# FFN of a decoder block in three chunks of hidden columns, with two of each eight pairs of contraction tiles as seven block products instead of eight

## The chip, the cores and the metric

The kernel runs on one core of one Trainium2 chip, as one launch. The metric is the device time of the launch in microseconds (us), as the median of several runs; lower is better.

## What is computed

One decoder block on 272 tokens (16 meta tokens, which the output drops, and 256 of the input) with a model width of 2,048, all in float32. Cut to what matters:

```python
hn = rms_norm(h, norm_mix_g)
u, gb_in, gc_in, v_in, ga_lin, gbr_lin = split(hn @ w_in)
y_a = grouped_matmul(causal_multiscale_pool(u), pool_w) * pool_scale
y_b = (gb_in * causal_depthwise_conv(gc_in * v_in, conv_w)) @ conv_out_w
g_a, g_b = split(sigmoid(concat(ga_lin, gbr_lin) + b_gate))
h = h + (g_a * y_a + g_b * y_b) @ w_o
hn = rms_norm(h, norm_ffn_g)
gate, up = split(hn @ w_gate_up)            # 2048 -> 2 x 5632
h = h + (silu(gate) * up) @ w_down          # 5632 -> 2048
out = rms_norm(h, norm_final_g)[:, 16:]
```

## The kernel before

**Matmuls in three passes.** A float32 operand is split into two parts, hi (rounded to the matmul's type) and lo (the rest), and a product is hi*hi + hi*lo + lo*hi: three matmuls of 128 x 128 by 512 columns that add up in one PSUM bank. In `mm_rows` (lines 149 to 155) the activations are the stationary operand (128 contraction rows x 128 tokens) and the weights the moving one (128 x 512 columns); lines 153, 154 and 155 are the three passes.

**The stream of weights.** All weights lie in memory in the order of use, as chunks of eight 128 x 128 tiles (512 KB). `load` (line 101) brings one into one of 5 raw buffers, on SP's queue. `split_weights` (line 108) makes hi on ScalarE (line 115) and lo on VectorE (line 116) into a ring of 3 hi and 3 lo tiles. `next_tile` and `next_block` call `advance` at each new chunk, which issues loads up to 4 chunks ahead and splits up to 2 ahead. A chunk is two blocks of 512 columns, so in the row-wise stages it feeds 2 contraction tiles x 2 token halves x 3 passes = 12 matmuls.

**The stages.** First the input projection and the two mixers, with the weights stationary (`pair`, `flat`, lines 189 to 200). Then, row-wise by `rows` (line 157): gates and mixers' outputs in 4 column chunks, the output projection in 4 (line 412), FFN up in FC = 11 chunks of 512 gate and 512 up columns (lines 437 to 448), and FFN down in 4 chunks of 512 columns over all FT = 44 contraction tiles (lines 464 and 465). `rows` takes one bank for each of the two token halves and steps through the contraction tiles; banks rotate among 8. The results of a stage lie by token, and the next needs them by contraction: `turn` (line 234) transposes them on TensorE (line 242) and `narrow` or `split` (lines 212 to 222) make hi and lo. `turn_a(c - 1)` stands between the gate and the up half of chunk c; the last turn of a stage stands `BW` = 4 contraction tiles ahead of the end of the first row pass of the next (argument `before`), which needs its result at once.

**Around it.** The FFN norm is applied late: `r2`, one over the root mean square, is found after the output projection and multiplied into the gate and up sums (lines 441, 442, 447). In FFN down every chunk is added to `hn` (line 467 by `binary`, line 209), squared on ScalarE (468) and multiplied by the final gain on GpSimd, for the last chunk on VectorE (469). In the last chunk `HELD` = 6 contraction tiles are done for token half 0 first and then for half 1, so that the first half's scaling and its store lie beside matmuls.

What sets the order: a scheduler of the framework orders each engine's instructions when the kernel is built, by the written order and by what is ready; at run time each engine keeps that order.

Of the kernel before, what the change touches and what calls it, by code (L numbers as in the profile page):

```python
# [31 lines left out]
LOADS_AHEAD = 4  # L32
SPLITS_AHEAD = 2
# [14 lines left out]
SPAD = 34  # L48
# [5 lines left out]
def block_kernel(ctx: ExitStack, tc: tile.TileContext, xT, xn, gfin, consts, spread, weights, out):  # L54
# [3 lines left out]

    nc = tc.nc
# [3 lines left out]
    wraw = ctx.enter_context(tc.tile_pool(name="wraw", bufs=5))  # L63
    whi = ctx.enter_context(tc.tile_pool(name="whi", bufs=3))
    wlo = ctx.enter_context(tc.tile_pool(name="wlo", bufs=3))
    ps = ctx.enter_context(tc.tile_pool(name="ps", bufs=8, space=PSUM))
    scope = ExitStack()
    spool = scope.enter_context(tc.tile_pool(name="spool", bufs=KT))
# [13 lines left out]
    def bank():  # L82
        return ps.tile([P, 512], F32, name="acc")
# [14 lines left out]
    raws, splits = {}, {}  # L98
# [9 lines left out]
    def split_weights(c, parts=1):  # L108
        raw = raws.pop(c)
        hi = whi.tile([P, CH * P], F32R, name="hi")  # L110
        lo = wlo.tile([P, CH * P], F32R, name="lo")
        step = CH * P // parts
        for s in range(0, CH * P, step):
            q = slice(s, s + step)
            nc.scalar.copy(out=hi[:, q], in_=raw[:, q])  # L115
            nc.vector.tensor_tensor(out=lo[:, q], in0=raw[:, q], in1=hi[:, q], op=ALU.subtract)  # L116
        splits[c] = hi, lo

    state = {"tile": 0, "loaded": 0, "split": 0}

    def advance(c):
        while state["loaded"] < min(c + LOADS_AHEAD + 1, n_chunks):
            load(state["loaded"])
            state["loaded"] += 1
        while state["split"] < min(c + SPLITS_AHEAD + 1, n_chunks):
            split_weights(state["split"])
            state["split"] += 1

    def next_tile():
        c, i = divmod(state["tile"], CH)  # L130
        if i == 0:
            advance(c)
            splits.pop(c - 1, None)
        state["tile"] += 1
        hi, lo = splits[c]
        return hi[:, i * P : (i + 1) * P], lo[:, i * P : (i + 1) * P]

    def next_block():
        c, i = divmod(state["tile"], CH)
        assert i % BW == 0  # L140
        if i == 0:
            advance(c)
            splits.pop(c - 1, None)
# [82 lines left out]
    slots = {"a": 20, "b": 16, "x": 8}  # L226

    def slot(tag, shape, dt=F32):
        return apool.tile(shape, dt, name="act", tag=tag, bufs=slots[tag])
# [4 lines left out]
    def turn(src, c, make):  # L234

        for j in range(0, BW, 2):
            p = bank()
            for i in range(2):
                for b in range(NB):
                    q = i * SEQ + b * P  # L240
                    f = slice((j + i) * P, (j + i + 1) * P)
                    nc.tensor.transpose(out=p[:, q : q + P], in_=src[b][:, f], identity=ident)  # L242
            for i in range(2):
                make(c * BW + j + i, p[:, i * SEQ : (i + 1) * SEQ])
# [47 lines left out]
    for c in range(KT * HEAD // CH):  # L292
        k0 = c * CH // HEAD
        k1 = k0 + CH // HEAD
        xsp += [wide(xall[:, k, :], col(C_GMIX, k)) for k in range(k0, k1)]
        split_weights(c, 2 if c == 0 else 1)
        state["split"] = c + 1
# [72 lines left out]
    def turn_s(c):  # L370
        turn(s_rows.pop(c), c, lambda j, p: ss.append(narrow(p, "a")))
# [28 lines left out]
    hpool = scope.enter_context(tc.tile_pool(name="hpool", bufs=KT))  # L400
    tmr = scope.enter_context(tc.tile_pool(name="tmr", bufs=1))
    hn = one.tile([P, NB, D], F32, name="hn", tag="stream")
    nc.gpsimd.dma_start(out=hn, in_=xn)
    sq2 = one.tile([P, NB, NC], F32, name="sq2")
    r2 = one.tile([P, NB], F32, name="r2")
    hsp = []

    def turn_h(c):
        turn([hn[:, b, c * BC : (c + 1) * BC] for b in range(NB)], c,
             lambda j, p: hsp.append(split(hpool.tile([P, 2, SEQ], F32R, name="hp"), p, col(C_GFFN, j))))  # L410

    for c in range(NC):
        for b, p in enumerate(rows(ss, n=KT, before=(lambda: turn_s(NC - 1)) if c == 0 else None)):
            h = hn[:, b, c * BC : (c + 1) * BC]
            binary(h, p, h, ALU.add)
            junk = tmr.tile([P, BC], F32, name="junk", tag="row", bufs=4)
            nc.scalar.activation(out=junk, in_=h, func=AF.Square, accum_out=sq2[:, b, c : c + 1])
        if c > 0:
            turn_h(c - 1)
    st2 = one.tile([P, NB, SPAD], F32, name="st2")  # L420
    for b in range(NB):
        ms, sd, y, y2, m2 = [st2[:, b, i : i + 1] for i in range(5)]
        binary(ms, sq2[:, b, 0:1], sq2[:, b, 1:2], ALU.add)
        binary(ms, ms, sq2[:, b, 2:3], ALU.add)
        binary(ms, ms, sq2[:, b, 3:4], ALU.add)
        mean(ms, ms)
        rsqrt(r2[:, b : b + 1], ms, sd, y, y2, m2)


    acts, a_rows = [], {}  # L430

    def turn_a(c):
        order = [t for t in slots for _ in range(slots[t])]
        turn(a_rows.pop(c), c, lambda j, p: acts.append(narrow(p, order[j])))

    for c in range(FC):
        gs = []
        for b, p in enumerate(rows(hsp, n=KT, before=(lambda: turn_h(NC - 1)) if c == 0 else None)):
            r = r2[:, b : b + 1]
            g = tmr.tile([P, BC], F32, name="gs", tag="row", bufs=4)  # L440
            nc.scalar.activation(out=g, in_=p, func=AF.Sigmoid, scale=r)
            nc.vector.scalar_tensor_tensor(out=g, in0=p, scalar=r, in1=g, op0=ALU.mult, op1=ALU.mult)
            gs.append(g)
        if c > 0:
            turn_a(c - 1)
        for b, p in enumerate(rows(hsp)):
            nc.vector.scalar_tensor_tensor(out=gs[b], in0=p, scalar=r2[:, b : b + 1], in1=gs[b], op0=ALU.mult, op1=ALU.mult)
        a_rows[c] = gs


    first = rows(acts, n=FT, before=lambda: turn_a(FC - 1))
    scope.close()
    fin = ctx.enter_context(tc.tile_pool(name="fin", bufs=1))
    gf = fin.tile([P, D], F32, name="gf")
    nc.gpsimd.dma_start(out=gf, in_=gfin)
    hg = fin.tile([P, NB, D], F32, name="hg")
    junk = fin.tile([P, BC], F32, name="junk")
    part = fin.tile([P, NB, NC], F32, name="part")
    base = fin.tile([P, NB], F32, name="base")
    st = fin.tile([P, NB, 6], F32, name="st")  # L460
    preload = fin.tile([P, 1], F32, name="preload")
    for c in range(NC):
        q = slice(c * BC, (c + 1) * BC)
        last = c == NC - 1
        for b, p in enumerate(first if c == 0 else rows(acts, HELD if last else 0)):
            h = hn[:, b, q]
            binary(h, p, h, ALU.add)
            nc.scalar.activation(out=junk, in_=h, func=AF.Square, accum_out=part[:, b, c : c + 1])
            (nc.vector if last else nc.gpsimd).tensor_tensor(out=hg[:, b, q], in0=h, in1=gf[:, q], op=ALU.mult)
            if c == 0 and b == 1:  # L470
                nc.scalar.activation(out=preload, in_=ones[:, 0:1], func=AF.Sqrt)
            if c == NC - 2:

                s = base[:, b : b + 1]
# [89 lines left out]
```

## Time and profile before

| | |
|---|---|
| runs | 1491.25 us median of 3 (1491.2 to 1491.41) |
| profiled execution | 1491.44 us |
| its span | 1489.6 us |
| TensorE matmul / weight load busy | 1478.4 us / 1276.2 us |
| VectorE / ScalarE / GpSimd busy | 861.3 / 656.8 / 15.6 us |
| read from memory | 285.38 MB |

The span goes from the first to the last instruction of the profiled execution; its time has 1.84 us around it. Matmuls are pipelined: each one's recorded time covers its way through the array, so recorded times of neighbours overlap and add up to more than the span would hold. What one costs is seen from the distance of the starts.

### The profile page before, as it was taken

Reading aid. Unit: us, or ns where it says so; the run is one execution under the profiler, and the core shown is the slowest. Engines: PE = TensorE matmul, PEld = TensorE weight load, DVE = VectorE, ACT = ScalarE, POOL = GpSimd, SP = SyncE. Lnnn points to the kernel's source line nnn. Section 1 sums busy time; section 2 is a strip of 40 time slices with the busy share of each in tenths; the row PEclk is TensorE's granted clock in tenths of the full one; section 3 lists DMA queues with packets and bytes.
Section 4 is the critical chain, followed back from the end, with each engine's and each line's share of the span. In section 5 each row is a group of like instructions: output and inputs, shape, how many; then the busy total and the mean of one; then the engine's idle time right before and its main releaser. Section 6 shows DMA issues by size and latency. Waiting matters only on the chain.

```text
span 1489.6 us, 19622 instructions
## 1 busy us (share of the span) xinstructions
PE 1478.4 (99%) x7796; PEld 1276.2 (86%) x7796; DVE 861.3 (58%) x1020; ACT 656.8 (44%) x785; POOL 15.6 (1%) x18
## 2 busy tenths in 40 slices
PE   9999999999999999999999999999999999999997
PEld 9999999999888888888888888888888888888886
DVE  7986666666555555555565555555555554445454
ACT  6544444444444444444454444444344444344343
POOL 0000000000000000000000000000000000000000
PEclk9999999999999999999999999999999999999999
DMA  9555555555765655565556555556555556566553
GB/s 338 186 187 184 184 184 185 185 185 186 235 215 188 207 196 193 188 196 186 183 175 197 193 184 191 191 185 196 186 191 189 186 192 219 181 198 196 193 192 125
DMA packets 79403, 288.76 MB, mean 194 GB/s; under 512 B 8912, under 2 KB 9168, under 8 KB 79056
## 3 DMA queue, kind: packets, MB, share of 16 engines
q1 hardware_dynamic: 77472, 279.61, 57.4%
q0 software_dynamic: 1120, 6.29, 1.3%
q10 hardware_dynamic: 720, 1.61, 0.3%
q8 instruction: 61, 1.00, 0.3%
q14 instruction: 30, 0.25, 0.0%
HBM read 285.38 MB, written 2.10 MB: 193 GB/s over the span
## 4 chain that ended last, share of the span: by engine, by line
PE 98%; ACT 1%; DMA 0%; DVE 0%; ACTq 0%; issue 0%
PE acc L153 24%; PE acc L155 24%; PE acc L154 24%; PE acc L186 6%; PE acc L185 6%; PE acc L187 6%; PE acc L179 4%; PE acc L180 2%; PE acc L242 1%; PE acc L307 0%; PE acc L305 0%; PE acc L306 0%; DMA raw<-weights 0%; ACT hi L115 0%; DVE lo L116 0%; ACT hg L486 0%
## 5 line engine op out<-in xcount | busy, mean ns | idle before, releaser
L116 DVE TENSOR_TENSOR lo<-raw,hi 128x1024 fp32r<-128x1024 f32 (+1 forms) x529 | 648.2, 1226 | 580.0 <-ACT hi L115 576.8
L115 ACT CAST hi<-raw 128x1024 fp32r<-128x1024 f32 (+1 forms) x529 | 555.5, 1050 | 789.8 <-PE acc L155 558.5
L153 PE MATMUL acc<-hi,hp 128*128 128x512 f32 x704 | 274.9, 391 | 0.3 <-ACT hi L115 0.3
L154 PE MATMUL acc<-lo,hp 128*128 128x512 f32 x704 | 273.9, 389 | 0.0
L155 PE MATMUL acc<-hi,hp 128*128 128x512 f32 x704 | 273.9, 390 | 0.0
L153 PE MATMUL acc<-hi,act 128*128 128x512 f32 x640 | 248.9, 390 | 0.5 <-ACT hi L115 0.5
L154 PE MATMUL acc<-lo,act 128*128 128x512 f32 x640 | 248.8, 389 | 0.0
L155 PE MATMUL acc<-hi,act 128*128 128x512 f32 x640 | 248.5, 389 | 0.0
L186 PE MATMUL acc<-xp,hi 128*128 128x258 f32 (+3 forms) x704 | 198.8, 282 | 0.0
L185 PE MATMUL acc<-xp,hi 128*128 128x258 f32 (+3 forms) x704 | 198.6, 282 | 0.0
L187 PE MATMUL acc<-xp,lo 128*128 128x258 f32 (+3 forms) x704 | 198.5, 282 | 0.0
L155 PEld LDWEIGHTS acc<-hi,hp 128*128 128x128 f32 x704 | 132.2, 188 | 27.6
L153 PEld LDWEIGHTS acc<-hi,hp 128*128 128x128 f32 x704 | 132.1, 188 | 27.4 <-ACT hi L115 0.5
L154 PEld LDWEIGHTS acc<-lo,hp 128*128 128x128 f32 x704 | 132.2, 188 | 27.1
L153 PEld LDWEIGHTS acc<-hi,act 128*128 128x128 f32 x640 | 120.0, 188 | 25.7 <-ACT hi L115 1.0
L154 PEld LDWEIGHTS acc<-lo,act 128*128 128x128 f32 x640 | 120.2, 188 | 25.0
L155 PEld LDWEIGHTS acc<-hi,act 128*128 128x128 f32 x640 | 120.2, 188 | 24.8
L185 PEld LDWEIGHTS acc<-xp,hi 128*128 128x128 f32 x704 | 132.6, 188 | 0.7
L187 PEld LDWEIGHTS acc<-xp,lo 128*128 128x128 f32 x704 | 132.6, 188 | 0.0
L186 PEld LDWEIGHTS acc<-xp,hi 128*128 128x128 f32 x704 | 132.5, 188 | 0.0
L153 PE MATMUL acc<-hi,xp 128*128 128x512 f32 x256 | 100.0, 391 | 0.0
L155 PE MATMUL acc<-hi,xp 128*128 128x512 f32 x256 | 99.7, 389 | 0.0
(106 smaller groups left out, 1006.5 us busy)
## 6 DMA issues: line engine op xcount, KB each, us to landing
raw<-weights SPq DMA_DIRECT2D x527, 512.0 KB, 3.4
sp<-spread POOLq DMA_DIRECT2D x4, 768.0 KB, 6.2
hn<-xn POOLq DMA_DIRECT2D x1, 2048.0 KB, 9.7
xall<-xT SPq DMA_DIRECT2D x7, 272.0 KB, 7.4
gf<-gfin POOLq DMA_DIRECT2D x1, 1024.0 KB, 7.1
out<-hg SPq DMA_DIRECT2D x2, 512.0 KB, 2.6
out<-hg ACTq DMA_DIRECT2D x2, 512.0 KB, 3.5
raw<-weights ACTq DMA_DIRECT2D x2, 256.0 KB, 5.1
```

What stands on the lines that cost most here:

```text
L115: nc.scalar.copy(out=hi[:, q], in_=raw[:, q])
L116: nc.vector.tensor_tensor(out=lo[:, q], in0=raw[:, q], in1=hi[:, q], op=ALU.subtract)
L153: nc.tensor.matmul(out=p, lhsT=a[:, 0, t], rhs=hi, start=first, stop=False)
L154: nc.tensor.matmul(out=p, lhsT=a[:, 0, t], rhs=lo, start=False, stop=False)
L155: nc.tensor.matmul(out=p, lhsT=a[:, 1, t], rhs=hi, start=False, stop=last)
L179: nc.tensor.matmul(out=p, lhsT=hi, rhs=a[:, :, off : off + SEQ], start=first, stop=False)
L180: nc.tensor.matmul(out=p[:, :SEQ], lhsT=lo, rhs=a[:, 0, off : off + SEQ], start=False, stop=last)
L185: nc.tensor.matmul(out=p, lhsT=hi, rhs=a[:, 0, off : off + n], start=first, stop=False)
L186: nc.tensor.matmul(out=p, lhsT=hi, rhs=a[:, 1, off : off + n], start=False, stop=False)
L187: nc.tensor.matmul(out=p, lhsT=lo, rhs=a[:, 0, off : off + n], start=False, stop=last)
L242: nc.tensor.transpose(out=p[:, q : q + P], in_=src[b][:, f], identity=ident)
```

## The change

It rewrites the FFN, and what feeds it.

- **Groups and units.** A *group* covers 1,024 columns (up: 512 gate and 512 up columns of one chunk; down: 1,024 output columns) and both token halves, in four "plain" banks. It steps through *pairs* of contraction tiles. The first and the fourth step of each group (`plan_of`, `STRASSEN = 2`) are *units*: seven block products of 128 tokens x 256 contraction x 512 columns in place of eight. Three go straight into plain banks, four (`p1, p5, p6, p7`) into product banks of their own; after the second unit of a group four operations combine these, and the results are added in at the group's end. The other pairs are done as before, 24 matmuls each.
- **Operands of a unit.** On the token side `pair_forms` makes four 128-column sums beside the four blocks, in `turn`. On the weight side `split_weights` takes two raw chunks, makes four 512-column sums on VectorE and splits seven blocks into hi and lo: one cut of 512 columns and three of 1,024, in four ring tiles.
- **Ring.** From the output projection on a second ring of 3 is used, 6 tiles in all; a job (plain chunk 1 tile, unit 4) is split as soon as its tiles fit beside those held. Loads run 5 chunks ahead of the cuts.
- **Three chunks.** The FFN hidden columns are done in chunks of 4, 4 and 3 x 512: the up groups of a chunk, then two down groups over its 16, 16 or 12 contraction tiles, which add to `hn`. So there are 11 up groups and 4 down groups of 8 pairs, and 2 down groups of 6.
- **Norm and turns.** The rows of `hn` are scaled by an estimate of the norm from three of four column chunks before they are turned; the exact ratio `rest` is multiplied in after. Turns 0 to 2 of the FFN input stand in the last row pass of the output projection (`early_turns`). `turn_a` of the chunk before stands ahead of step m = 5 of an up group, and for the last up group of a FFN chunk ahead of the step of the first down group that needs it.
- **End.** The final gain is multiplied in on VectorE. In the last group `HELD` = 2 pairs are done bank by bank.

Its core (further hunks: renamed arguments, the two bank tags, pools for the new tiles):

```diff
-LOADS_AHEAD = 4
-SPLITS_AHEAD = 2
+RAWS = 5
+RING = 3
...
+    def part(j):
+        used = [sum(1 for _, h in held_tiles if h == i) for i in range(len(homes))]
+        i = used.index(min(used))
+        assert used[i] < RING
+        held_tiles.append((j, i))
+        return (homes[i][0].tile([P, CH * P], F32R, name="hi"), homes[i][1].tile([P, CH * P], F32R, name="lo"))
...
+            r0, r1_ = raws.pop(c), raws.pop(c + 1)
+            b12, b11, b22, b21 = r0[:, :BC], r0[:, BC:], r1_[:, :BC], r1_[:, BC:]
+            ta = sums.tile([P, 2 * BC], F32, name="ta")
+            td = sums.tile([P, 2 * BC], F32, name="td")
+            (ah, al), (bh, bl), (ch, cl), (dh, dl) = [part(j) for _ in range(4)]
+            nc.vector.tensor_tensor(out=ta[:, :BC], in0=b11, in1=b12, op=ALU.add)
+            cut(bh[:, :BC], bl[:, :BC], b11)
+            nc.vector.tensor_tensor(out=ta[:, BC:], in0=b12, in1=b22, op=ALU.add)
+            nc.vector.tensor_tensor(out=td[:, :BC], in0=ta[:, :BC], in1=b22, op=ALU.add)
+            nc.vector.tensor_tensor(out=td[:, BC:], in0=td[:, :BC], in1=b21, op=ALU.add)
+            cut(ah, al, ta)
+            cut(dh, dl, td)
+            cut(ch, cl, r1_)
...
+    def advance(j):
+        held_tiles[:] = [h for h in held_tiles if h[0] >= j]
+        splits.pop(j - 1, None)
+        while True:
+            while state["loaded"] < min(state["cut"] + RAWS, n_chunks):
+                load(state["loaded"])
+                state["loaded"] += 1
+            r = state["ready"]
+            if r == len(jobs) or len(held_tiles) + jobs[r][0] > RING * len(homes):
+                return
+            split_weights(r)
...
+        f = tmr.tile([P, 8, P], F32, name="f", tag="f", bufs=1)
+        pv = p.rearrange("p (i b t) -> p i b t", i=2, b=NB)
+        for i, dst in enumerate((f[:, 0:8:7, :], f[:, 1:3, :])):
+            if g[i] is None:
+                nc.scalar.copy(out=dst, in_=pv[:, i])
+            else:
+                nc.scalar.activation(out=dst, in_=pv[:, i], func=AF.Copy, scale=g[i])
+        binary(f[:, 3], f[:, 7], f[:, 2], ALU.subtract)
+        binary(f[:, 5], f[:, 0], f[:, 7], ALU.subtract)
+        binary(f[:, 4], f[:, 3], f[:, 0], ALU.subtract)
+        binary(f[:, 6], f[:, 1], f[:, 4], ALU.add)
...
+    def early_turns():
+        for c in range(NC - 1):
+            h_rows_of(c)
+            turn_h(c)
...
+    def mm3(p, a, w, first, last):
+        (ah, al), (wh, wl) = a, w
+        nc.tensor.matmul(out=p, lhsT=ah, rhs=wh, start=first, stop=False)
+        nc.tensor.matmul(out=p, lhsT=ah, rhs=wl, start=False, stop=False)
+        nc.tensor.matmul(out=p, lhsT=al, rhs=wh, start=False, stop=last)
...
+        plain = {k: bank("c") for k in ("11", "12", "21", "22")}
+        prods = {k: bank("q") for k in ("p1", "p5", "p6", "p7")}
+        banks = {**plain, **prods}
...
+        extra, kept = None, []
+        for i, (m, s) in enumerate(plan):
+            if m in late:
+                late.pop(m)()
+            if s:
+                w = take()
+                for key, a, b in UNIT:
+                    add(key, forms[m][a], w[b])
+            else:
+                for k in range(2):
+                    w = take()
+                    if i < len(plan) - held:
+                        plain_step(forms[m], k, w, ("11", "12", "21", "22"))
+                    else:
+                        kept.append((forms[m], k, w))
+            if s and all(not x for _, x in plan[i + 1 :]):
+                e = {k: slot("x", [P, BC]) for k in plain}
+                nc.scalar.copy(out=e["11"], in_=prods["p1"])
+                binary(e["12"], prods["p6"], e["11"], ALU.add)
+                binary(e["21"], prods["p7"], e["12"], ALU.add)
+                binary(e["12"], prods["p5"], e["12"], ALU.subtract)
+                binary(e["22"], prods["p5"], e["21"], ALU.subtract)
+                extra = e
...
+    def gate_up(c, late):
+        plain, e, _, _ = group(hf, plan_of(KT // 2), late)
+        rest = [st2[:, b, 3:4] for b in range(NB)]
+        out_ = []
+        for b in range(NB):
+            g, u = e[f"{b + 1}1"], e[f"{b + 1}2"]
+            binary(g, plain[f"{b + 1}1"], g, ALU.add)
+            sg = tmr.tile([P, BC], F32, name="sg", tag="row", bufs=2)
+            nc.scalar.activation(out=sg, in_=g, func=AF.Sigmoid, scale=rest[b])
+            binary(u, plain[f"{b + 1}2"], u, ALU.add)
+            nc.vector.scalar_tensor_tensor(out=g, in0=g, scalar=rest[b], in1=sg, op0=ALU.mult, op1=ALU.mult)
+            nc.vector.scalar_tensor_tensor(out=g, in0=u, scalar=rest[b], in1=g, op0=ALU.mult, op1=ALU.mult)
+            out_.append(g)
...
+            late = {}
+            if c == 0:
+                late[KT // 2 - 2] = lambda: turn_h(NC - 1, "q")
+            elif i > 0:
+                late[KT // 2 - 3] = lambda c=c, i=i: turn_a(c - 1, af, 2 * (i - 1))
+            gate_up(c, late)
...
+        for g in range(NC // 2):
+            late = {2 * n - 2: lambda: turn_a(c - 1, af, 2 * (n - 1))} if g == 0 else {}
+            ends = last and g == NC // 2 - 1
+            plain, e, kept, step = group(af, plan_of(2 * n), late, HELD if ends else 0)
+            keys = [f"{b + 1}{i + 1}" for b in range(NB) for i in range(2)]
+            for key in keys:
+                b, cb = int(key[0]) - 1, 2 * g + int(key[1]) - 1
+                h = hn[:, b, cb * BC : (cb + 1) * BC]
+                binary(h, h, e[key], ALU.add)
+            for key in keys:
+                b, cb = int(key[0]) - 1, 2 * g + int(key[1]) - 1
+                h = hn[:, b, cb * BC : (cb + 1) * BC]
+                for f, k, w in kept:
+                    step(f, k, w, (key,))
+                binary(h, plain[key], h, ALU.add)
+                if last:
+                    finish(b, cb)
...
+HELD = 2
+STRASSEN = 2
+CHUNKS = (4, 4, 3)
+FORMS = ("a11", "a12", "a22", "s1", "s2", "s3", "s4", "a21")
+UNIT = (("p1", "a11", "b11"), ("p5", "s1", "t1"), ("p6", "s2", "t2"), ("p7", "s3", "t3"),
+        ("11", "a12", "b21"), ("12", "s4", "b22"), ("21", "a22", "t4"))
...
+    for m in range(STRASSEN):
+        plan.append((m, True))
+        plan += [(plain.pop(0), False) for _ in range(2)]
+    return plan + [(m, False) for m in plain]
```

## Rows read from the trace of the kernel before

**Rows 1.** the page, parts 1 and 2: busy us (share), calls; GB/s by slice

```profile
PE 1478.4 (99%) x7796; PEld 1276.2 (86%) x7796; DVE 861.3 (58%) x1020; ACT 656.8 (44%) x785; POOL 15.6 (1%) x18
...
GB/s 338 186 187 184 184 184 185 185 185 186 235 215 188 207 196 193 188 196 186 183 175 197 193 184 191 191 185 196 186 191 189 186 192 219 181 198 196 193 192 125
```

**Rows 2.** the page's part 4, chain that ended last: shares by engine, by line

```profile
PE 98%; ACT 1%; DMA 0%; DVE 0%; ACTq 0%; issue 0%
PE acc L153 24%; PE acc L155 24%; PE acc L154 24%; PE acc L186 6%; PE acc L185 6%; PE acc L187 6%; PE acc L179 4%; PE acc L180 2%; PE acc L242 1%; PE acc L307 0%; PE acc L305 0%; PE acc L306 0%; DMA raw<-weights 0%; ACT hi L115 0%; DVE lo L116 0%; ACT hg L486 0%
```

**Rows 3.** groups by line and form: busy us, mean ns, idle before; then loads

```profile
L116 DVE TENSOR_TENSOR lo<-raw,hi 128x1024 fp32r<-128x1024 f32 x527 | 646.9, 1228 | 578.8 <-ACT hi L115 575.6
L115 ACT CAST hi<-raw 128x1024 fp32r<-128x1024 f32 x527 | 554.2, 1052 | 788.5 <-PE acc L155 558.5 <-PE acc L186 108.5 <-issue 66.0
...
L217 DVE TENSOR_TENSOR act<-acc,act 128x256 fp32r<-128x256 f32 x60 | 23.8, 418 | 1.8 <-ACT act L216 1.8
...
L442 DVE SCALAR_TENSOR_TENSOR gs<-acc,r,gs 128x512 f32<-128x512 f32 x22 | 15.8, 751 | 5.3 <-ACT gs L441 5.3
...
L220 DVE SCALAR_TENSOR_TENSOR hp<-acc,cst,hp 128x256 fp32r<-128x256 f32 x16 | 7.3, 480 | 2.6 <-ACT hp L219 2.6
...
L209 DVE TENSOR_TENSOR act<-act,sp 128x512 f32<-128x512 f32 x8 | 5.2, 686 | 0.7 <-ACT act L378 0.7
...
L116 DVE TENSOR_TENSOR lo<-raw,hi 128x512 fp32r<-128x512 f32 x2 | 1.4, 692 | 1.3 <-ACT hi L115 1.2
...
raw<-weights SPq DMA_DIRECT2D x527, 512.0 KB, 3.4
```

**Rows 4.** timeline of PE, FFN up: start us, us, engine, line, operation

```profile
845.79 0.39 PE L153 MATMUL acc<-hi,hp 128*128 128x512 f32 x1
...
848.51 0.39 PE L153 MATMUL acc<-hi,hp 128*128 128x512 f32 x1
```

**Rows 5.** FFN up, down: PE, PEld, DVE, ACT, POOL busy; clock, DMA, GB/s

```profile
751.10:1239.90 488.80, 488.54 (x2199) 405.21 (x2198) 262.40 (x278) 216.40 (x254) 0.00 (x0) 1.00 0.58 189
...
1239.90:1480.00 240.10, 239.84 (x1063) 198.56 (x1062) 118.16 (x113) 98.21 (x108) 11.15 (x7) 1.00 0.57 184
```

**Rows 6.** timelines of ACT and DVE, FFN up; bracketed: idle before, releaser

```profile
848.71 1.05 ACT L115 CAST hi<-raw 128x1024 fp32r<-128x1024 f32 x1 [1.67 <-PE acc L155]
...
849.80 1.23 DVE L116 TENSOR_TENSOR lo<-raw,hi 128x1024 fp32r<-128x1024 f32 x1 [1.50 <-ACT hi L115]
```

**Rows 7.** timeline of DVE in the pooling stage, with work queued

```profile
61.98 1.22 DVE L116 TENSOR_TENSOR lo<-raw,hi 128x1024 fp32r<-128x1024 f32 x1
63.11 0.42 DVE L217 TENSOR_TENSOR act<-pl,act 128x256 fp32r<-128x256 f32 x1
63.45 0.42 DVE L322 TENSOR_TENSOR win<-u 128x259 f32<-128x259 f32 x1
63.91 0.43 DVE L322 TENSOR_TENSOR win<-win 128x257 f32<-128x257 f32 x1
```

**Rows 8.** timeline of PE at turns: not needed at once, needed at once

```profile
817.71 1.03 PE L242 MATMUL acc<-ident,gs 128*128 128x128 f32 x8
818.50 0.48 PE L153 MATMUL acc<-hi,hp 128*128 128x512 f32 x1
...
767.25 1.04 PE L242 MATMUL acc<-ident,hn 128*128 128x128 f32 x8
768.55 0.97 PE L153 MATMUL acc<-hi,hp 128*128 128x512 f32 x3 [0.26 <-ACT hi L115]
```

**Rows 9.** timelines at the end: PE's last matmul, ScalarE's last scaling

```profile
1480.81 0.39 PE L155 MATMUL acc<-hi,act 128*128 128x512 f32 x1
...
1483.98 1.15 ACT L486 ACTIVATE hg<-hg,st 128x1024 f32<-128x1024 f32 x1 [0.87 <-DVE st L260]
```

**Rows 10.** timeline of ACT at a turn of FFN activations

```profile
863.16 1.06 ACT L115 CAST hi<-raw 128x1024 fp32r<-128x1024 f32 x1
864.16 0.65 ACT L216 CAST act<-acc 128x256 fp32r<-128x256 f32 x2
```

More of the change, by code (lines that the diff above doesn't have):

```diff
@@ L47 @@
 CPAD = 96
-SPAD = 34
+SPAD = 38
 TPAD = 320
@@ L106, in load @@
         raws[c] = raw
[L108 to L127, printed above, removed]
+    jobs, held_tiles, splits = job_list(n_chunks), [], {}
+    homes = [(whi, wlo)]
+    def part(j):
[4 more added lines that the diff above has]
+        return (homes[i][0].tile([P, CH * P], F32R, name="hi"), homes[i][1].tile([P, CH * P], F32R, name="lo"))
@@ new lines, in cut, with split_weights @@
+    def cut(hi, lo, raw):
+        nc.scalar.copy(out=hi, in_=raw)
+        nc.vector.tensor_tensor(out=lo, in0=raw, in1=hi, op=ALU.subtract)
+    def split_weights(j, parts=1):
+        kind, c = jobs[j]
+        if kind == 1:
+            raw = raws.pop(c)
+            hi, lo = part(j)
+            step = CH * P // parts
+            for s in range(0, CH * P, step):
+                q = slice(s, s + step)
+                cut(hi[:, q], lo[:, q], raw[:, q])
+            splits[j] = hi, lo
+        else:
[12 more added lines that the diff above has]
+            cut(ch, cl, r1_)
+            splits[j] = {"b11": (bh[:, :BC], bl[:, :BC]),
+                         "t1": (ah[:, :BC], al[:, :BC]), "t3": (ah[:, BC:], al[:, BC:]),
+                         "t2": (dh[:, :BC], dl[:, :BC]), "t4": (dh[:, BC:], dl[:, BC:]),
+                         "b22": (ch[:, :BC], cl[:, :BC]), "b21": (ch[:, BC:], cl[:, BC:])}
+        state["ready"] = j + 1
+        state["cut"] = c + (1 if kind == 1 else 2)
@@ L404, in block_kernel, with h_rows_of @@
     sq2 = one.tile([P, NB, NC], F32, name="sq2")
[L405 to L410, printed above, removed]
+    st2 = one.tile([P, NB, SPAD], F32, name="st2")
+    hf, h_rows = {}, {}
+    def h_rows_of(c):
+        h_rows[c] = []
+        for b in range(NB):
+            r = slot("x", [P, BC])
+            nc.scalar.activation(out=r, in_=hn[:, b, c * BC : (c + 1) * BC], func=AF.Copy, scale=st2[:, b, 1:2])
+            h_rows[c].append(r)
@@ L436, in block_kernel @@
[L436 to L448, printed above, removed]
@@ L451, in block_kernel @@
[L451 to L461, printed above, removed]
@@ L462, in block_kernel @@
[L462 to L470, printed above, removed]
-                nc.scalar.activation(out=preload, in_=ones[:, 0:1], func=AF.Sqrt)
-            if c == NC - 2:
-                s = base[:, b : b + 1]
-                binary(s, part[:, b, 0:1], part[:, b, 1:2], ALU.add)
-                binary(s, s, part[:, b, 2:3], ALU.add)
-                mean(s, s)
-            if last:
-                ms, sd, y, y2, m2, r = [st[:, b, i : i + 1] for i in range(6)]
-                nc.vector.scalar_tensor_tensor(out=ms, in0=part[:, b, c : c + 1], scalar=1.0 / D, in1=base[:, b : b + 1],
+        rsqrt(r, ms, sq, y, y2, m2)
@@ new lines, in block_kernel, with take @@
+        binary(rest, s, sd)
+        nc.vector.tensor_scalar(out=rest, in0=rest, scalar1=-1.0, scalar2=2.0, op0=ALU.mult, op1=ALU.add)
+        binary(rest, rest, sd)
+        binary(rest, rest, r)
+    state["job"] = state["tile"] // CH
+    def take():
+        j = state["job"]
+        advance(j)
+        state["job"] += 1
+        return splits[j]
+    def mm3(p, a, w, first, last):
[3 more added lines that the diff above has]
+        nc.tensor.matmul(out=p, lhsT=al, rhs=wh, start=False, stop=last)
```

177 lines of the change are left out of this document (140 added, 37 removed).

## Prediction

> **What bounds the kernel now.** I read the page first. TensorE is busy 99% of the span, VectorE 58% and ScalarE 44% [rows 1], and the chain that ended last is TensorE for 98% of the span, 72% in the three matmul lines of the row-wise stages [rows 2], where the 2,112 FFN-up and 1,056 FFN-down matmuls stand. So a matmul that goes away takes time with it, as long as nothing else becomes late. Busy time is no price for a matmul: each one is recorded with 0.39 us, but two of one line that lie twelve matmuls apart start 2.72 us apart [rows 4]. One 512-column matmul thus costs 2.72 / 12 = 0.2267 us, and I use this pitch everywhere. It closes the books: a FFN-up chunk has 192 matmuls, 43.52 us, and eight transposes, 0.9 us more, and eleven of them fill the 488.8 us of that stage [rows 5], 44.44 each. In that stage VectorE is busy 262 of 488.8 us and in the down stage 118 of 240 [rows 5]; it mostly waits for the hi half from ScalarE, and ScalarE for TensorE to free a ring tile [rows 3, 6]. That spare time is what the change spends.
>
> **What it removes.** A unit of two contraction tiles, two token halves and 1,024 columns takes 8 block products of 3 matmuls now and 7 after: 24 becomes 21. There are two units in each of 11 up groups and in each of 6 down groups, 34 in all, so 34 x 3 = 102 matmuls go: 102 x 0.2267 = 23.1 us. The Trainium skill, TensorE: Matmul & The Clock Gate, Back-to-back issue gap, gives about 131 ns per 512-column matmul in a sustained stream; by it the 102 would be worth an estimated 13.4 us. The trace's 0.2267 us disagrees, and is used.
>
> **What it adds, per unit, on VectorE** (durations of [rows 3], SBUF sums as act<-act,sp). Four 512-column sums 4 x 0.686, one 512-column lo half 0.692 and three 1,024-column lo halves 3 x 1.228: 7.12 us, where two plain chunks cost 2.46. A sum that reads PSUM I price at 0.686 too. Combining the products adds four a group, 2.74. Up: four sums and four scalar operations at its end, 4 x 0.686 + 4 x 0.751 = 5.75 (before: the scalar ones only). Down: eight sums, 5.49. For one up group: 2 units 14.24, 12 plain chunks 14.74, combining 2.74, end 5.75, turning four tiles 1.67: **39.1 us of VectorE against 186 x 0.2267 + 0.9 = 43.1 us of TensorE**. A down group over eight pairs: 37.2 against 42.2. One over six pairs (third FFN chunk): 14.24 + 9.82 + 8.23 = 32.3 against 138 x 0.2267 = 31.3, and its first has the turn (1.67) and four products with the final gain, moved here from POOL (4 x 0.69): 36.7 against 32.2. In the three groups that turn the two unit pairs of a chunk, each pair needs four 128-column sums and two 512-column lo halves in place of four 256-column ones. A 128-column operation is not shown; its bounds are 0.21 (half of the 256-column one) and 0.418 (all of it) [rows 3], and 0.29 continues the step from 512 to 256 columns: 2 x (4 x 0.29 + 2 x 0.69) = 5.1 for 1.67, so 42.5 of 43.1.
>
> Those sums are high. Where VectorE has work queued, a 1.22 us operation and its follower start 1.13 us apart, 0.42 us ones 0.34 apart, and a step that needs the one before it 0.46 apart [rows 7]. With 0.085 us less for each of 44 operations the up group is 35.4, with forms 38.1, the first six-pair group 33.0. The Trainium skill, VectorE: DVE Perf Modes, The DRAIN you can't avoid, speaks against the change here: it has each operation wait until the pipe is empty, which gives the full sums, though another section of the page lets an operation that nothing holds start earlier. The trace agrees with the wait for dependent steps only.
>
> **Whether units are ready in time.** The ring holds six hi/lo tiles, a unit takes four, so its split is emitted only when two plain chunks, 5.44 us of TensorE, remain in front. The last of the four tiles comes free 0.2 us after such a boundary (the hi cast starts 0.2 us behind the first matmul of the next chunk [rows 4, 6]); then come hi 1.05 and two lo halves, 2.46: 3.7 of 5.44 us, and the last pieces are used only 12 matmuls into the unit. This holds if sums and first cuts (4.66 us) ran before, in the three chunks, 8.2 us, between the last plain split of a group, emitted six tiles ahead, and that boundary, when no other split is emitted. The second ring lies where the mixers' operands were; its first casts wait for their last matmul and are done (0.2 + 1.05 + 1.23) 2.5 us later, two chunks, 5.4 us, before use: nothing, and 2.5 without that cover. ScalarE, at 1.052 for each 1,024-column hi and no more for a smaller one [rows 3], has under 25 us of a group's 43. Banks: a group holds all eight; the next begins on the four product banks, read empty in mid-group, and needs the first plain bank 2.72 us later, the last after 4.76; the up group's eight end operations by pitch take about 5 us, with the fourth bank read after some 3.4: no cost, cover about 1 us. SP's loads now run five chunks ahead of the cuts; a unit takes two raw buffers and frees the second only after its last cut, but a load lands in 3.4 us [rows 3] and the stage draws 189 GB/s where the start drew 338 [rows 5, 1]: nothing, and without that cover one landing, 3.4 us, per late unit. On POOL's queue the gain load waits for the freed pool, 30 us ahead of need: nothing.
>
> **What it moves.** A turn whose result is needed at once costs more than one that is not: from the first transpose to the next matmul 1.30 us instead of 0.79 [rows 8], and about 0.1 in the matmuls after. I count 0.6. Before there are three such turns, the last in FFN down; after, two stay and FFN down has one in each of three chunks: 2 x 0.6 = 1.2. The first three turns of the FFN input move into the last four contraction steps of the output projection: 24 transposes (3 x 0.9 us) and 5.4 us of matmuls cover them, while VectorE has 12.7 us (one lo 1.23, two unit pairs 5.1, eight halves of 0.480 [rows 3], a chunk 1.23, two adds 1.37); what the first unit needs is half of that. Bounds 0 and 12.7 - 8.1 = 4.6; I take 0.5, as only the excess needed first counts. The first six-pair group: bounds 0.8 (33.0) and 4.5 (36.7 against 32.2); I take 1, since VectorE there has work queued as in [rows 7]. The end is unchanged: from the last matmul to the end of the span 8.4 us, which is the sum, the square, the root, the last scaling and the store [rows 9].
>
> **Sum**, against the profiled execution's own 1491.44 (span 1489.6, 1.84 around it): - 23.1 + 1.2 + 0.5 + 1.0 = **1471.0**. The median of the runs is 0.2 lower; allowing three units one late hand-over each, 0.26 [rows 8], I say **1471.5 us**.
>
> **Rivals.**
> VectorE falls behind: it costs full durations and each unit starts one hand-over late, 0.26 us as in [rows 8]: 34 x 0.26 = 8.8, the first six-pair group 4.5, turns and edge 1.7: 1491.4 - 23.1 + 15.0 = 1483. For it: 32.3 against 31.3. Against: the pitches of [rows 7], and six tiles of lead. The Trainium skill, VectorE: DVE Perf Modes, The DRAIN you can't avoid, would have this case; the rows bear it out for part of the operations.
> Slower: the split of a unit becomes the path. The place is the cut that waits for a ring tile: if nothing of the split runs ahead of it, the last lo comes 0.2 + 1.05 + 7.12 = 8.4 us after the boundary, with two plain splits in front of the second unit of a group (2.46) 10.9, where it is needed after 5.44 + 2.72 = 8.2. The lo half before it is needed 1.36 earlier and comes 1.23 earlier, so the first unit of a group loses some 0.4 and the second 2.9: mean 1.65 x 34 = 56, time 1491.4 - 23.1 + 56 = 1524. It decides from 23.1 / 34 = 0.68 us per unit. For it: a lo half is always held until the ring tile is free [rows 6]. Against: the built order need not be the written one, since a chunk's hi cast stands in front of two casts of a turn that is written ahead of it [rows 10], so sums can run ahead; and VectorE idles 579 us ahead of its lo halves [rows 3].
> No change: the stream of weights sets the pace, so removing matmuls does nothing: 1491. Against: the FFN's draw of 189 GB/s is little over half of the start's 338 [rows 1, 5].
>
> **Chances.** Forecast (1468 to 1476) 0.68; full-duration VectorE (1476 to 1488) 0.15; gain eaten or pace of the stream (1488 to 1494) 0.05; slower 0.09; below 1468, if a cost of before that I do not see goes too, 0.03. About 0.2%, 3 us, is what a measurement of this kernel tells from no change, so faster 0.86, same 0.05, slower 0.09. Without any stall the time is 1491.25 - 23.1 = 1468.1, so the range starts at 1467.5; it runs to 1484, past the full-duration case, which leaves out the slower cases and a rest.
>
> **What would show it.** Right: 102 fewer 512-column matmuls at the same pitch; up groups of 43.1 us; VectorE near 80 to 90% in the FFN; TensorE's waits for lo or hi under 5 us in all. Wrong: TensorE idle ahead of the first product of units, released by VectorE (full-duration or ring rival), most in the six-pair groups; a pitch above 0.23; or a lower granted clock in the FFN.

## The result, and the profile after

The changed kernel takes **1468.55 us** (median of 4 runs, 1468.22 to 1469.23) against 1491.33 us for the one before on the same chips: a ratio of 0.9848, 95% interval 0.9831 to 0.9865. That is 22.8 us less. The forecast was 1471.5 us with a range from 1467.5 to 1484. The profiled execution took 1468.22 us, with a span of 1466.4 us.

The page of the kernel after, in the order of [rows 1] and [rows 2]: busy time and counts, VectorE's tenths in 40 slices, GB/s by slice, and the chain's shares.

```profile
PE 1455.9 (99%) x7694; PEld 1256.1 (86%) x7694; DVE 1091.4 (74%) x1426; ACT 733.7 (50%) x899; POOL 4.9 (0%) x12
...
DVE  7986666666656565656588888877888887788898
...
GB/s 337 186 189 185 187 187 188 184 185 182 228 220 188 219 188 189 190 196 229 187 148 209 175 215 215 193 180 195 199 182 215 215 190 182 194 196 186 215 215 115
...
PE 98%; DVE 1%; ACT 1%; DMA 0%; ACTq 0%; issue 0%
```

TensorE has 7796 - 7694 = 102 matmuls fewer, and it is still 98% of the chain. VectorE went from 861 to 1091 us; its tenths rise from 5 and 6 to 7, 8 and 9 from the middle of the span on, where the FFN stands. The stream of weights flows as before.

The views of stretches, columns as in [rows 5]. The first row is nearly the whole FFN, the second one up group in steady state.

```profile
753.00:1461.00 708.00, 704.97 (x3153) 582.87 (x3151) 606.40 (x783) 383.43 (x464) 0.55 (x1) 1.00 0.59 193
...
820.00:863.00 43.00, 43.00 (x196) 35.70 (x195) 38.66 (x53) 25.03 (x31) 0.00 (x0) 1.00 0.60 196
```

VectorE is busy 606.4 / 708 = 86% of the FFN, and TensorE is fully busy beside it. Where did the added VectorE work go? Into the idle time ahead of its lo halves. In the waits of VectorE between 753 and 1455 us, first of the kernel before and then of the one after (us in total, times, longest), the wait for the hi half shrank from 324 to 83 us:

```profile
DVE lo L116 <- ACT hi L115: 324.0, 237, 1.5
```

```profile
DVE lo L130 <- ACT hi L129: 82.9, 77, 1.6
DVE ta L149 <- DMA raw<-weights: 10.1, 17, 1.0
DVE ta L151 <- DMA raw<-weights: 4.7, 8, 1.6
```

TensorE's own waits from 740 us on are its weight loads' only, in the same columns. Each stands for a few tenths of a microsecond, 2.5 us in all, and a part of it lies beside matmuls that still ran:

```profile
PEld acc L543 <- ACT act L261: 0.9, 3, 0.3
PEld acc L543 <- DVE hn L254: 0.7, 2, 0.5
PEld acc L543 <- ACT hp L264: 0.4, 1, 0.4
PEld acc L545 <- DVE act L262: 0.3, 2, 0.2
PEld acc L544 <- DVE lo L130: 0.2, 1, 0.2
```

Groups of the kernel after, columns as in [rows 3]: the new operations (the weight side's four sums, L149 to L153, a lo half of sums and the 128-column sums of the token side).

```profile
L130 DVE TENSOR_TENSOR lo<-raw,hi 128x1024 fp32r<-128x1024 f32 x493 | 598.2, 1221 | 281.1 <-ACT hi L129 278.4
...
L130 DVE TENSOR_TENSOR lo<-td,hi 128x1024 fp32r<-128x1024 f32 x34 | 41.6, 1223 | 23.3 <-ACT hi L129 22.8
...
L149 DVE TENSOR_TENSOR ta<-raw 128x512 f32<-128x512 f32 x34 | 23.4, 689 | 10.7 <-DMA raw<-weights 10.6
...
L254 DVE TENSOR_TENSOR f<-f 128x128 f32<-128x128 f32 x32 | 8.3, 286 | 0.9 <-ACT f L304 0.6
```

The durations are those that the prediction took (0.686, 1.228, and 0.29 for the form that no row showed).

**Closing the books of the FFN.** The timeline of PE after has the first and the last FFN matmul at 750.37 and 1457.61 us, 707.2 us apart:

```profile
750.37 0.39 PE L543 MATMUL acc<-hi,hp 128*128 128x512 f32 x1
...
1457.61 0.39 PE L545 MATMUL acc<-hi,act 128*128 128x512 f32 x1
```

Of the counts and prices in the prediction, 3,066 matmuls x 0.2267 = 695.1 and 12 turns x 0.9 = 10.8 make 705.9. All stalls of the FFN together are thus 1.3 to 1.4 us. For the kernel before, from 750.82 to [rows 9] 1480.81, the same sum gives 3,168 x 0.2267 + 10.8 = 729.0 of 730.0: 1.0 us. The 102 matmuls went at their full price, and 0.4 us of stalls came in return.

### The profile page after: what moved, and what is told of

Read it like the earlier page. It is cut to its first block, busy times and chain, and to the rows that moved or that the text cites. A ratio compares the mean times of both kernels' runs of the same rounds, so it can differ in the third digit from the quotient of the medians.

```text
span 1466.4 us, 19960 instructions
## 1 busy us (share of the span) xinstructions
PE 1455.9 (99%) x7694; PEld 1256.1 (86%) x7694; DVE 1091.4 (74%) x1426; ACT 733.7 (50%) x899; POOL 4.9 (0%) x12
## 4 chain that ended last, share of the span: by engine, by line
PE 98%; DVE 1%; ACT 1%; DMA 0%; ACTq 0%; issue 0%
PE acc L543 16%; PE acc L545 16%; PE acc L544 16%; PE acc L199 8%; PE acc L198 8%; PE acc L200 8%; PE acc L231 6%; PE acc L230 6%; PE acc L232 6%; PE acc L224 4%; PE acc L225 2%; PE acc L288 1%; PE acc L378 0%; PE acc L376 0%; PE acc L377 0%; DMA raw<-weights 0%
## 5 line engine op out<-in xcount | busy, mean ns | idle before, releaser
L130 DVE TENSOR_TENSOR lo<-raw,hi 128x1024 fp32r<-128x1024 f32 (+1 forms) x529 | 621.6, 1185 | 284.7 <-ACT hi L129 282.1
L129 ACT CAST hi<-raw 128x1024 fp32r<-128x1024 f32 (+1 forms) x529 | 537.3, 1023 | 559.7 <-PE acc L200 174.2
L543 PE MATMUL acc<-hi,hp 128*128 128x512 f32 x682 | 266.1, 391 | 0.1
L544 PE MATMUL acc<-lo,hp 128*128 128x512 f32 x682 | 265.4, 389 | 0.0
L545 PE MATMUL acc<-hi,hp 128*128 128x512 f32 x682 | 264.8, 389 | 0.0
L543 PEld LDWEIGHTS acc<-hi,hp 128*128 128x128 f32 x682 | 128.0, 188 | 27.4 <-DVE hn L254 0.7
L545 PEld LDWEIGHTS acc<-hi,hp 128*128 128x128 f32 x682 | 128.0, 188 | 26.7
L544 PE MATMUL acc<-lo,act 128*128 128x512 f32 x340 | 132.4, 389 | 0.0
L543 PE MATMUL acc<-hi,act 128*128 128x512 f32 x340 | 132.3, 391 | 0.0
L545 PE MATMUL acc<-hi,act 128*128 128x512 f32 x340 | 131.9, 389 | 0.0
L199 PE MATMUL acc<-lo,xp 128*128 128x512 f32 x256 | 99.6, 389 | 0.0
L224 PE MATMUL acc<-xp,hi 128*128 128x512 f32 x256 | 91.1, 398 | 0.0
L254 DVE TENSOR_TENSOR act<-acc,act 128x512 f32<-128x512 f32 x128 | 85.2, 682 | 0.1
## 6 DMA issues: line engine op xcount, KB each, us to landing
hn<-xn POOLq DMA_DIRECT2D x1, 2048.0 KB, 10.8
```

The lines of the kernel that those rows point to most:

```text
L129: nc.scalar.copy(out=hi, in_=raw)
L130: nc.vector.tensor_tensor(out=lo, in0=raw, in1=hi, op=ALU.subtract)
L199: nc.tensor.matmul(out=p, lhsT=a[:, 0, t], rhs=lo, start=False, stop=False)
L224: nc.tensor.matmul(out=p, lhsT=hi, rhs=a[:, :, off : off + SEQ], start=first, stop=False)
L543: nc.tensor.matmul(out=p, lhsT=ah, rhs=wh, start=first, stop=False)
L544: nc.tensor.matmul(out=p, lhsT=ah, rhs=wl, start=False, stop=False)
```

## The experiments

Each is an edit of the changed kernel; "against after" means against 1468.55 us. Ratios are to the kernel before, which took 1491.23 to 1491.33 us in the three rounds of runs. The theory is that TensorE's matmuls, at 0.2267 us each, set the time and VectorE's work is hidden; the rivals are that VectorE's load or the ring's lead sets it.

**The eighth product put back.**

```diff
-        total.update({k: 2 * (len(plan) - n_s) + (n_s if k != "22" else 0) for k in plain})
+        total.update({k: 2 * (len(plan) - n_s) + n_s for k in plain})
...
                     add(key, forms[m][a], w[b])
+                add("22", forms[m]["a22"], w["b22"])
```

The fourth plain bank so holds one product too many; all the sums and splits of a unit stay.

> The changed kernel with an eighth product put back into each of the 34 units (second token half times the fourth weight block, added to the fourth bank, so that bank holds more than the reference asks): 102 matmuls of 512 columns more, everything on VectorE, ScalarE and the queues as it is. TensorE theory (time is the number of these matmuls times the pitch of 0.2267 us): 1468.5 + 23.1 = 1491.6, between 1490.5 and 1492. Rival, VectorE paces the groups and TensorE has hidden slack: well below that, 1468 to 1480. Rival, the gain came from the new order of chunks, turns and ring and not from the products: 1468 to 1472.

Measured: 1493.05 us (1492.27 to 1493.7), ratio 1.0011, interval 1.0002 to 1.002. That is 24.5 us against after, for 102 matmuls worth 23.1, and 1.05 above the upper end of what was expected. The rest of about 1.4 us is in TensorE's timeline at two turns of FFN down (0.77 and 0.62 us over the pitch); the first of them:

```profile
964.45 0.40 PE L544 MATMUL acc<-lo,act 128*128 128x512 f32 x1
965.45 0.96 PE L545 MATMUL acc<-hi,act 128*128 128x512 f32 x3 [0.59 <-DVE act L262]
```

What follows: with all its new VectorE work and none of its saving, the kernel is 1.8 us above the one before, 0.1%. So the new order and the sums bring no gain of their own, and the gain is the matmuls'. With TensorE's full time back the sums and splits are hidden; that they are in the change too is what the waits and the books above show. The small waits at turns that the prediction allowed for do exist, in another order of instructions than the one that was built for the change.

**One unit a group instead of two** (`STRASSEN = 1`).

> The changed kernel with one unit in each group instead of two: 17 units, 51 matmuls more, and 17 x 4.66 us less on VectorE. TensorE theory: 1468.5 + 51 x 0.2267 = 1480.1, within 1 us. Rival, VectorE paces the groups: less than 5 us more, as its load falls. Rival, order and ring: 1468 to 1472.

Measured: 1479.60 us (1479.53 to 1480.09), ratio 0.9923, interval 0.9908 to 0.9937. Against after, 51 more matmuls cost 11.05 us, 0.217 each; half of the units give half of the gain.

**A third unit in the up groups**, twice: as the pair `m` = 2 with a plan that has it sixth, and as the pair 5 in the same place, whose token side is turned later.

```diff
+def plan_up():
+    return [(0, True), (3, False), (4, False), (1, True), (5, False), (2, True), (6, False), (7, False)]
...
-                late[KT // 2 - 3] = lambda c=c, i=i: turn_a(c - 1, af, 2 * (i - 1))
+                late[KT // 2 - 2] = lambda c=c, i=i: turn_a(c - 1, af, 2 * (i - 1))
```

> The changed kernel with three units in each of the 11 up groups (two in the down groups as now): 33 matmuls fewer, and by row durations VectorE 39.1 + 4.7 = 43.8 us in an up group where TensorE has 42.4, by the pitch of a queue that never runs empty 39.6. TensorE theory with VectorE at its pitch cost and the ring early enough: 1468.5 - 7.5 = 1461. Rival, VectorE is at its end with two units and costs its durations: each up group takes 43.8 and more, 11 x 0.8 = 9 us over the two-unit kernel, 1476 or above. In between, the third unit stands one pair behind the second, so its split has the three chunks of lead less: 1463 to 1470 with TensorE waiting ahead of the third unit.

Measured: 1466.83 us (1465.29 to 1467.86), ratio 0.9835, interval 0.9818 to 0.9851. Of the 7.5 us that 33 matmuls are worth, 1.7 arrived. That lies in the range expected for waits ahead of the third unit, but the waits are not there. In the steady up groups TensorE never waits (43.00 of 43.00 us in the stretch from 820 to 863, VectorE 40.91). The loss is at one place, the end of the output projection. Its rows in TensorE's timeline:

```profile
758.08 0.88 PE L543 MATMUL acc<-hi,hp 128*128 128x512 f32 x2 [3.16 <-ACT hi L129]
...
760.35 0.63 PE L543 MATMUL acc<-hi,hp 128*128 128x512 f32 x1
760.77 0.63 PE L544 MATMUL acc<-lo,hp 128*128 128x512 f32 x1
```

And the stretches over the wait and behind it:

```profile
754.00:758.00 4.00, 0.92 (x4) 0.39 (x3) 4.00 (x12) 4.00 (x11) 0.00 (x0) 1.00 0.38 133
759.50:763.00 3.50, 3.50 (x10) 2.71 (x10) 3.35 (x14) 1.68 (x4) 0.00 (x0) 0.54 0.79 248
```

Three early turns now make token-side sums for three pairs, and from 754 to 758 us VectorE and ScalarE are both busy 4.00 of 4.00 us while TensorE waits. Then comes a second cost: in the next stretch the granted clock is 0.54, about the lower of the two levels (1.2 of 2.4 GHz), and the starts lie 0.42 us apart instead of 0.227. The four runs fit this: the one with a mean granted clock of 0.999, as in the change's runs (0.998 to 0.999), took 1465.29 us, and the three with 0.996 or 0.997 took 1466.68 to 1467.86. So I took a pair that is turned later:

```diff
+    return [(0, True), (2, False), (3, False), (1, True), (4, False), (5, True), (6, False), (7, False)]
```

> Three units in the up groups as in the run with three units, but the third is the contraction pair 5 in place of 2, so that at the edge of the output projection the forms of a third pair no longer stand in front of the pairs that the first group needs first; the turn stands behind the third unit. Theory (what the earlier run lost was one stall at that edge, 3.2 us of waiting and 8 matmuls at half the clock): 1468.5 - 33 x 0.2267 = 1461.1, at most 1 us more. Rival (VectorE at 93 to 99% is what the earlier run ran into): 1465 to 1468 again.

Measured: 1460.97 us (1460.89 to 1461.1), ratio 0.9797, interval 0.9782 to 0.9811. Against after 7.6 us for 33 matmuls, the whole price. The loss in the first form was that edge, not VectorE's load in the groups: their plan is the same but for which pair is the unit.

**Three units also in the four down groups of eight pairs** (two more token tiles, in the pool of the weight side's sums; for lack of room one norm tile moves to a new pool that closes earlier).

```diff
+    if n == 8:
+        return [(0, True), (2, False), (3, False), (1, True), (4, False), (5, True), (6, False), (7, False)]
...
-        af = {"order": iter(["a"] * slots["a"])}
+        af = {"order": iter(["a"] * slots["a"] + ["y"] * 2), "n": n}
```

> As the last, and with a third unit in the four down groups of eight pairs too (two token-side tiles more, in a pool of the FFN stage; one early vector lies in another pool): 12 matmuls fewer again, VectorE 41.9 us by durations and about 38 by the pitch against 41.5. Theory: 1461.1 - 2.7 = 1458.4, at most 1.5 more. Rival, VectorE late in the down groups: 1460 or above.

Measured: **1458.57 us** (1458.4 to 1459.06), ratio 0.9781, interval 0.9765 to 0.9798. It is the fastest of all, 10 us below the change. Its row for the stretch from 780 to 1340 us has VectorE busy 534 of 560 us, 95%, with TensorE still at 559.7:

```profile
780.00:1340.00 560.00, 559.68 (x2507) 463.61 (x2506) 534.18 (x681) 317.86 (x379) 0.00 (x0) 1.00 0.59 199
```

**The ring with five tiles instead of six.** This is the slower rival's place: the lead of a unit's split.

```diff
-            if r == len(jobs) or len(held_tiles) + jobs[r][0] > RING * len(homes):
+            if r == len(jobs) or len(held_tiles) + jobs[r][0] > (RING if len(homes) == 1 else 5):
```

> The changed kernel with five of the six ring tiles used in the FFN stage: a unit is split when one plain chunk (2.72 us) remains in front of it, and only one plain chunk is split ahead while a unit runs. If the lead of six tiles is what keeps units off the path: the chunks behind a unit come late by what VectorE does in front of them, 0.3 to 1 us at 34 units, 1479 to 1502. Rival, VectorE's spare time alone decides and the lead does not matter: 1468 to 1470.

Measured: 1478.18 us (1478.08 to 1480.47), ratio 0.9916, interval 0.9901 to 0.9931: 9.6 us against after, with the same instructions to do, and just under the 1479 to 1502 expected. TensorE's waits from 740 us on (the largest of its matmuls, then of its weight loads) name the lo halves:

```profile
PE acc L544 <- DVE lo L130: 2.7, 5, 0.8
...
PEld acc L544 <- DVE lo L130: 7.5, 14, 1.2
```

One such place in its timeline:

```profile
845.33 0.50 PE L544 MATMUL acc<-lo,hp 128*128 128x512 f32 x1 [0.76 <-DVE lo L130]
```

Three steps of the chain that ends in this wait, from the view of the critical path, and VectorE's wait for the weights of its first sums between 753 and 1455 us:

```profile
833.40 4.50 DMA raw<-weights
...
837.93 0.69 DVE ta L149
...
844.14 1.14 DVE lo L130
```

```profile
DVE ta L149 <- DMA raw<-weights: 29.0, 29, 2.0
```

What follows: the sixth tile is worth 9.6 us, some 40% of the gain, or 9.6 / 34 = 0.28 us per unit on average; in the timeline the loss stands at some fourteen places, the edge and the turns among them. TensorE does wait for lo halves, as in the slower rival. But loads run a fixed number of chunks ahead of the cuts, so later cuts load later too: at the place shown VectorE, in its built order, first waits for a chunk to land and then does the end of a group ahead of the lo half, and over the FFN such waits of first sums are 29.0 us against 10.1 in the change. This run does not tell the lead of the splits from that of the loads.

**VectorE loaded further.** Idle 512-column sums, which nobody reads, written between the plain steps of each group: four in the first kernel, and in the second one per chunk, 12 in a group of eight pairs and 8 in one of six.

```diff
                     w = take()
+                    if k == 0 and i in (1, 2, 4, 5):
+                        binary(bal[:, 0], bal[:, 1], bal[:, 1], ALU.add)
```

> The changed kernel with four idle sums of 512 columns added on VectorE to each of the 17 groups, one beside each of the first plain steps' pairs (nobody reads them): 4 x 0.60 = 2.4 us more at the pitch, where VectorE was busy 35.3 to 38.7 us of an up group's 43. Theory (TensorE sets the time, VectorE's unused time absorbs load): no change, 1468 to 1470. Rival (VectorE's idle time is waits that a load only pushes along): + 2.4 x 17 = 41 us, or a good part of it, above 1475.

Measured: 1471.28 us (1470.72 to 1472.81), ratio 0.9867, interval 0.9853 to 0.9882.

> The same with one such sum at every plain chunk, 12 in a group of eight pairs and 8 in a group of six: 7.2 us at the pitch, so 43 to 46 us of VectorE against 43.1 of TensorE in the up groups and about 42 against 42.2 in the down groups. If VectorE's cost is its pitch, groups run over by 0 to 3 us: 1475 to 1500, and TensorE's waits stand at units. If its full durations count (8.2 us, 47 against 43): 17 x 4 = 68 us and more, above 1520. If it is not near the bound at all: 1468 to 1470.

Measured: 1473.51 us (1472.21 to 1474.57), ratio 0.988, interval 0.9865 to 0.9895. Both lie between the cases that were priced for them.

The sums need nothing of the groups that they are written in, and the built order has many of them ahead of the FFN. Busy time and counts of these sums alone (VectorE, then GpSimd, which fills their tile), in the first kernel and then in the second:

```profile
660.00:752.00 92.00, 40.55 (x59) 0.95 (x1) 1.00 0.56 189
```

```profile
660.00:752.00 92.00, 40.55 (x59) 0.52 (x1) 1.00 0.54 189
...
780.00:1340.00 560.00, 93.38 (x136) 0.00 (x0) 1.00 0.59 196
```

So 59 of the 68 sums of the first kernel run before the FFN, and it does not show what a loaded VectorE does in the groups. In the second, 136 of 196 run between 780 and 1340 us. Its stretches, then its VectorE's wait for the hi half between 753 and 1455 us:

```profile
780.00:1340.00 560.00, 558.63 (x2499) 461.64 (x2499) 547.49 (x710) 291.04 (x339) 0.00 (x0) 1.00 0.59 196
820.00:863.00 43.00, 43.00 (x196) 35.70 (x195) 42.87 (x61) 24.46 (x31) 0.00 (x0) 1.00 0.59 197
```

```profile
DVE lo L130 <- ACT hi L129: 10.9, 12, 1.5
```

VectorE is busy 42.87 of 43 us in the up group from 820 us on, and 547.5 / 560 = 97.8% over thirteen groups' time. TensorE loses 1.4 of 560 us there. By the distances of TensorE's starts, about 2.2 of the 5.0 us against after are lost at the same edge as above, and about 1.0 at each of two turns (787 and 1217 us); of the 2.7 us of the first kernel about 2.2 are lost at the edge. The first wait there, of TensorE for VectorE's sum of `hn`, is in both kernels the same to a hundredth, as is the number of idle sums that run ahead of it:

```profile
754.06 0.50 PE L545 MATMUL acc<-hi,hp 128*128 128x512 f32 x1 [1.58 <-DVE hn L254]
```

```profile
753.45 0.50 PE L545 MATMUL acc<-hi,hp 128*128 128x512 f32 x1 [1.58 <-DVE hn L254]
```

The full-duration price falls with the second kernel. The groups of VectorE from 780 to 1340 us, count times mean duration, add up to 599 us, more than the 560 that there are, and yet TensorE hardly waits. The same sum for the three units of eight is 583 us. The Trainium skill, VectorE: DVE Perf Modes, The DRAIN you can't avoid, says that the next operation does not start until the pipe is empty, and also that one that is not held starts earlier. The trace shows the earlier start where an operation needs nothing of the one before. In VectorE's timeline of the kernel after, a step that reads the result of the one before starts 0.72 us after it (the first two rows; its duration is 0.69), and two 1.22 us operations of which the second needs nothing of the first start 1.13 us apart (the last two):

```profile
846.47 0.68 DVE L152 TENSOR_TENSOR td<-ta,raw 128x512 f32<-128x512 f32 x1
847.19 0.69 DVE L153 TENSOR_TENSOR td<-td,raw 128x512 f32<-128x512 f32 x1
847.80 1.22 DVE L130 TENSOR_TENSOR lo<-ta,hi 128x1024 fp32r<-128x1024 f32 x1
848.93 1.22 DVE L130 TENSOR_TENSOR lo<-raw,hi 128x1024 fp32r<-128x1024 f32 x1
```

## Why the prediction was right, point by point

**What bounds the kernel** held: TensorE's start-to-start time. Five kernels with 45, 33 and 0 matmuls fewer and 51 and 102 more than the change lie at 1458.57, 1460.97, 1468.55, 1479.60 and 1493.05 us. The step per matmul is 0.217 to 0.240 us between each of them and the change, around the 0.2267 read from [rows 4]. The 131 ns of the Trainium skill (TensorE: Matmul & The Clock Gate, Back-to-back issue gap) are not borne out by any of these steps.

**What it removes** held: 23.1 us forecast. The profiled execution is 1491.44 - 1468.22 = 23.2 us shorter. In the FFN the count times the pitch went, less 0.4 us for stalls.

**What it adds** held. An up group with forms was put at 38.1 us of VectorE by pitches and 42.5 by durations, against 43.1 of TensorE; measured were 38.66 in 43. The two groups of six pairs, put at 33.0 for the first, had 30.6 of 32 us and 30.3 of 31, and all that TensorE waited there for a split was one weight load's 0.2 us.

**Whether units are ready in time** held: TensorE waits 0.2 us in all for a lo half. With one tile less it waits, as shown, for late loads as well as late splits. The landing of a chunk has become 4.2 us in place of 3.4 and VectorE's first sums wait 15 us in all for it, none of it passed on to TensorE.

**What it moves** is the term that was mis-sized, with the three late hand-overs: +3.5 us forecast, about zero measured. It makes up the 3 us between forecast and result. The step that failed is "two stay and FFN down has one in each of three chunks: 2 x 0.6 = 1.2". The written order has such turns, but the built order has other matmuls behind their transposes. The turn at 676 us in TensorE's timeline before:

```profile
676.01 1.04 PE L242 MATMUL acc<-ident,act 128*128 128x128 f32 x8
677.31 0.98 PE L153 MATMUL acc<-hi,act 128*128 128x512 f32 x3 [0.26 <-ACT hi L115]
```

Four places after: the same turn, one at the end of an up stage, the one of the first six-pair group, and the edge of the output projection.

```profile
675.96 1.04 PE L288 MATMUL acc<-ident,act 128*128 128x128 f32 x8
676.75 0.47 PE L198 MATMUL acc<-hi,act 128*128 128x512 f32 x1
...
954.73 1.04 PE L288 MATMUL acc<-ident,act 128*128 128x128 f32 x8
955.53 0.47 PE L543 MATMUL acc<-hi,act 128*128 128x512 f32 x1
...
956.07 0.40 PE L545 MATMUL acc<-hi,act 128*128 128x512 f32 x1
956.35 0.51 PE L543 MATMUL acc<-hi,act 128*128 128x512 f32 x1
...
1414.35 1.03 PE L288 MATMUL acc<-ident,act 128*128 128x128 f32 x8
1415.40 0.50 PE L543 MATMUL acc<-hi,act 128*128 128x512 f32 x1
...
751.50 0.39 PE L545 MATMUL acc<-hi,hp 128*128 128x512 f32 x1
751.98 0.50 PE L543 MATMUL acc<-hi,hp 128*128 128x512 f32 x1
```

- At 676 us the next matmul of the kernel before came 1.30 us behind the first transpose, as in [rows 8]; after, it comes 0.79 us behind. This turn lies ahead of the FFN, and with it the FFN starts 0.45 us earlier (750.37 instead of 750.82). Here 0.5 us was gained; I had counted the turn as staying.
- At 954.73 three matmuls follow 0.80 us behind the first transpose; the one at 956.35 comes 0.28 us behind its neighbour, not 0.227. Such a turn costs some 0.2 us in place of the 0.6; so does the one at 1211 us, and the last turn of the FFN's input, at 782 us, some 0.3.
- The first six-pair group: 1.05 us from transpose to matmul, 0.26 more than a turn that nobody waits for, in place of the 1.0 forecast.
- The edge: 0.48 us between two starts, so 0.25 lost and about 0.1 in the matmul after, in place of 0.5.

Over the pitch and an ordinary turn's 0.87 us, the turns and the edge after cost an estimated 1.4 us in all, from these starts, where the three turns before cost 1.6.

The lesson in it: I priced each turn by the worst one of the kernel before, though VectorE had room and the order is made anew for each kernel.

**The rivals.** Full-duration VectorE falls by the second loaded kernel and by the fastest one. The slower case, a unit's lo half that comes late, shows with five tiles, in part through late loads, and not with six. "No change" by the stream falls: the fastest kernel draws 199 GB/s where the change drew 197 in the same stretch.

**Left open.** How VectorE's bound looks beyond 98% wasn't tried. That the 59 idle sums ahead of the sum of `hn` make the 1.58 us wait in both loaded kernels is argued from their place and number, not tried by itself. How much of the 9.6 us of the fifth tile is late loads stays open. Why the turn at 676 us got its cover was not tried either.

## What to carry to other kernels

Where one engine is 98% of the chain and another idles in the same stretch, price the removed work by start-to-start distance and ask of the added work only two things: does it fit by pitch, and does its split have lead enough. Count the fit stage by stage, edges too: a third unit fitted in every group and still lost most of its gain at one hand-over between stages, until its token side was made later. Give a bursty producer one more buffer before judging it too slow; here one ring tile was 9.6 us, later loads included. And look in the trace where added load really ran: a kernel's written order is not its built order.

## What was not expected of the hardware

A single wait of 3.16 us on TensorE cost a second time through its clock. In the kernel with the third unit at pair 2, the granted clock reads 1.00 over the wait and 0.54 from 759.5 to 763 us, soon behind it; seven starts in a row lie 0.42 to 0.43 us apart, about 0.2 more than the pitch for each. Some eight matmuls ran so, which makes an estimated 1.6 us on top of the wait, from 0.2 x 8. Waits of under 2 us, as at the edge in the loaded kernels, show no such rows behind them.

VectorE could be kept 97.8% busy for 560 us, in the second loaded kernel, with TensorE losing 1.4 us of it. I had expected waits to appear well before that.
